# Dense products of a hybrid backbone step: upper and lower weight parts in two passes

## The chip, the core and the metric

The kernel runs on one core of one Trainium2 chip. The metric is device time in microseconds (us) of one execution. TensorE (PE in the profile, PEld for its weight loads) multiplies, VectorE (DVE), ScalarE (ACT) and GpSimd (POOL) work element by element, and SyncE (SP) issues nearly all transfers. Each engine works through its own instructions in order and waits on semaphores for the others.

## The reference, cut to what matters

One layer of a diffusion backbone for 128 context and 256 latent tokens, 384 columns in all, at width 1024 and in float32:

```python
h = _rmsnorm(x, p['norm_g'][0]) * (1.0 + sc1) + sh1
x = x + 0.5 * g1 * _swiglu(h, p['ffn_wi'][0], p['ffn_wo'][0])      # width 2816
h = _rmsnorm(x, p['norm_g'][1]) * (1.0 + sc2) + sh2
mix, states = _mixer_block(h, p, init, grid)                       # S5, SSD, gated DeltaNet
x = x + g2 * mix
h = _rmsnorm(x, p['norm_g'][2]) * (1.0 + sc3) + sh3
x = x + 0.5 * g3 * _swiglu(h, p['ffn_wi'][1], p['ffn_wo'][1])
```

The mixer projects `h` with `w_in` (the products' blocks of 128 columns), runs three scans in both directions, gates the branches and projects with `w_out`. Shifts, scales and gates come from SiLU(cond) @ `ada_w`.

## The kernel before

Activations lie transposed, features on the 128 partitions and the 384 tokens as columns (386 where two shift columns ride along). A dense product takes a weight tile of 128 output features by up to 8 slices of 128 input features from DRAM (`wraw`, three buffers) and splits it (`split_w`, lines 280 to 287): ACT casts it to the upper part `whi` in the fast float32r form (line 285), DVE subtracts that from the raw tile and leaves the lower part `wlo` (line 286). `whi` and `wlo` have two buffers each (`HLB`). Activations are split in the same way into `xh` and `xl` (`hh`/`hl`, `gh`/`gl`, and so on). `mm3` (lines 291 to 296) then adds three matmuls per slice k into one PSUM tile: upper weight by `xh` (line 294), upper weight by `xl` (line 295), lower weight by `xh` (line 296). A product of 8 slices is 24 matmuls.

There are 243 such products. In their order: the first FFN (`ffn(0, ...)`): per half of the 22 hidden blocks 22 products of `wi` (line 405; two to a block, multiplied on DVE at line 412) and 16 of `wo` (line 432; two to an output block, of 6 and 5 slices, added into `x` at line 434); then the mixer with 50 products of `w_in` (line 617) and one of small projections (line 631), 32 of the branches (line 1008) and 8 of `w_out` (line 1319); then the second FFN like the first. (Four more split tiles, of `wz`, lines 892 to 898, don't go through `mm3`.)

In the first FFN, DVE also computes the modulation vectors of later sections (line 272, a multiply with sum per 128x1024 tile) and tables for the S5 scan (lines 554 to 607, with a few transposes and matmuls on PE). In the mixer, DVE runs a recurrence of 31 steps (lines 828 to 838), PE transposes q, k and the convolved blocks through PSUM (`transposes`, line 695, two buffers that ACT empties, for q and k at line 825), and the inverses of the DeltaNet start with matmuls at lines 927 and 928, go on as small steps on DVE (lines 953 and 955), are written to DRAM (line 961) and read back (lines 1058 and 1060) for the matmuls at line 1045.

The order on each engine is not the order in which the code is written: the tile framework schedules by a simulated timeline, in which the next instruction that is ready goes first, and allots the buffers. So an edit in `mm3` can move instructions on every engine.

Of the kernel before, what the change touches and what calls it, by code (L numbers as in the profile page):

```python
# [22 lines left out]
KD = 8  # L23
# [118 lines left out]
def tile_hybrid(ctx: ExitStack, tc: tile.TileContext, a, o):  # L142
    nc = tc.nc
    V, S, G, PE = nc.vector, nc.scalar, nc.gpsimd, nc.tensor
# [32 lines left out]
    for q, names in enumerate((SMALL[:NFIRST], SMALL[NFIRST:])):  # L177
# [3 lines left out]
        for n in names:  # L181
            s = SMALL_SHAPES[n]
            w = int(np.prod(s))
# [104 lines left out]

    last_mm = [None]

    def mm3(pt, w, xh, xl, k0, nk, start, stop):
        hi, lo = w
        for k in range(nk):
            PE.matmul(pt, hi[:, k, :], xh[k0 + k], start=start and k == 0, stop=False)  # L294
            PE.matmul(pt, hi[:, k, :], xl[k0 + k], start=False, stop=False)  # L295
            last_mm[0] = PE.matmul(pt, lo[:, k, :], xh[k0 + k], start=False, stop=stop and k == nk - 1).ins  # L296

    def rsqrt(y, x, root=False):
# [93 lines left out]
    def ffn(f, xv, hh, hl, fill, rb=None, done=None, early=(), fill2=None):  # L392

        early = list(early)
        tw = T if rb is None else TW
        for part in range(2):
            gh, gl = blocks("gh", NH, FR), blocks("gl", NH, FR)
            for j in range(NH):  # L400
                m = part * NH + j
                pa, pb = ([psD, psD], [psD, psC], [psB, psB])[m if m < 3 else 0]
                pa, pb = pa([P, tw]), pb([P, tw])
                for w, pt in enumerate((pa, pb)):
                    mm3(pt, early.pop(0) if early else split_w(a["wi"][f, m, w], KD), hh, hl, 0, KD, True, True)
                sa = tmp.tile([P, T], F32, name="sa", tag="t384", bufs=NT3)
                g = tmp.tile([P, T], F32, name="g", tag="t384", bufs=NT3)
                if callable(rb):
                    rb = rb()
                if rb is None:  # L410
                    S.activation(sa, pa, AF.Silu)
                    V.tensor_tensor(g, sa, pb, op=ALU.mult)
                else:
                    V.tensor_tensor(sa, pa[:, 0:T], rb, op=ALU.mult)
                    V.tensor_tensor(g, pb[:, 0:T], rb, op=ALU.mult)
                    ba, bb = shifts(pa), shifts(pb)
                    for e, s0, s1 in HALVES:
                        S.activation(sa[:, s0:s1], sa[:, s0:s1], AF.Silu, bias=ba[:, e:e + 1])
                        V.scalar_tensor_tensor(g[:, s0:s1], g[:, s0:s1], bb[:, e:e + 1], sa[:, s0:s1],
                                               op0=ALU.add, op1=ALU.mult)  # L420
                S.copy(gh[j], g)
                last = V.tensor_tensor(gl[j], g, gh[j].bitcast(F32), op=ALU.subtract)
                with tc.issue_after(last.ins):
                    fill(m, g)
            if part == 0:
                gate = small.tile([P, KD, 2], F32, name="gate", tag="gate")
                V.tensor_scalar(gate, msec(2 if f == 0 else 8), 0.5, None, op0=ALU.mult)
            for m in range(KD):
                py = psd.tile([P, T], F32, name="ps_d", tag="ps_d")
                for k0, nk in ((0, 6), (6, 5)):  # L430
                    w = split_w(a["wo"][f, m, :, part * NH + k0:part * NH + k0 + nk], nk)
                    mm3(py, w, gh, gl, k0, nk, k0 == 0, k0 != 0)
                for e, s0, s1 in HALVES:
                    last = V.scalar_tensor_tensor(xv[m][:, s0:s1], py[:, s0:s1], gate[:, m, e:e + 1], xv[m][:, s0:s1],
                                                  op0=ALU.mult, op1=ALU.add)
                if fill2:
                    with tc.issue_after(last.ins):
                        fill2(part, m)
                if part == 1:
                    if m == 0:  # L440
                        acc = small.tile([P, T], F32, name="acc", tag="acc", bufs=1)
                    if f == 0 or m < KD - 1:
                        sq_add(acc, xv, m)
                    if done:
                        done(xv, m, acc)
        return acc
# [167 lines left out]

    def dense_in(blk, hh, hl, tw=T, ps=psD):
        pt = ps([P, tw])
        mm3(pt, split_w(a["win"][blk], KD), hh, hl, 0, KD, True, True)
        return pt

    def unscaled(dst, pt, rb):  # L620
# [80 lines left out]
    def mixer(es, xv, acc, xh, xl, sc):  # L701
# [53 lines left out]
        for m in range(4):  # L755
            pt = pts[m]
# [8 lines left out]
        hh, hl = modnorm(rb, sc, xv, 1)  # L765
# [33 lines left out]
        for which, tokt in ((1, ktok), (0, qtok), (2, vtok)):  # L799
            for m in range(4):  # L800
# [4 lines left out]
                pt = transposes([raw[:, X3[x]] for x in range(3)])  # L805
# [199 lines left out]

        def br(n, m, xh, xl):
            pt = psd.tile([P, T], F32, name="ps_d", tag="ps_d")
            mm3(pt, split_w(a["wbr"][m, n], 4), xh, xl, 0, 4, True, True)
            return pt

        def gates():
# [303 lines left out]
        for m in range(KD):  # L1315
            xo = t3("xo")
            nc.sync.dma_start(out=xo, in_=dX[m])
            py = psd.tile([P, T], F32, name="ps_d", tag="ps_d")
            mm3(py, split_w(a["wout"][m], KD), mgh, mgl, 0, KD, True, True)
            for e, s0, s1 in HALVES:  # L1320
                V.scalar_tensor_tensor(xv[m][:, s0:s1], py[:, s0:s1], gate2[:, m, e:e + 1], xo[:, s0:s1],
                                       op0=ALU.mult, op1=ALU.add)
# [110 lines left out]
```

## Time and profile before

| | us |
|---|---|
| median of 3 runs (1144.04 to 1144.78) | 1144.62 |
| profiled execution | 1144.53 |
| its span, first to last instruction | 1142.5 |
| PE busy | 1090.7 |
| PE weight loads busy | 1025.8 |
| DVE busy | 805.2 |
| ACT busy | 472.1 |
| POOL busy | 145.1 |

Matmuls are pipelined, so PE's busy time holds the end of one matmul beside the start of the next. Weight loads run beside the matmuls, one for each. The mean granted clock of TensorE is 0.987 of full speed.

### The profile page before, as it was taken

Reading aid. Unit: us, or ns where it says so; the run is one execution under the profiler, and the core shown is the slowest. Engines: PE = TensorE matmul, PEld = TensorE weight load, DVE = VectorE, ACT = ScalarE, POOL = GpSimd, SP = SyncE. Lnnn points to the kernel's source line nnn. Section 1 sums busy time; section 2 is a strip of 40 time slices with the busy share of each in tenths; the row PEclk is TensorE's granted clock in tenths of the full one; section 3 lists DMA queues with packets and bytes.
Section 4 is the critical chain, followed back from the end, with each engine's and each line's share of the span. In section 5 each row is a group of like instructions: output and inputs, shape, how many; then the busy total and the mean of one; then the engine's idle time right before and its main releaser. Section 6 shows DMA issues by size and latency. Waiting matters only on the chain.

```text
span 1142.5 us, 19011 instructions
## 1 busy us (share of the span) xinstructions
PE 1090.7 (95%) x7192; PEld 1025.8 (90%) x7192; DVE 805.2 (70%) x1652; ACT 472.1 (41%) x871; POOL 145.1 (13%) x135
## 2 busy tenths in 40 slices
PE   5999999999899999899899999999999999999996
PEld 2699899999899999799788888999899999999996
DVE  5699988899967759745554567786866974455554
ACT  5354323333355666743333232243444342334341
POOL 0000000000000100036172563116200000000000
PEclk9999999999999999899999999999999999999998
DMA  9787777576574653268646434456745634544342
GB/s 357 281 265 234 226 232 247 178 225 197 147 262 152 158 171 114 74 189 254 182 144 181 116 105 118 141 158 200 247 142 166 205 112 126 147 115 125 106 127 81
DMA packets 106731, 200.29 MB, mean 175 GB/s; under 512 B 34960, under 2 KB 60816, under 8 KB 106384
## 3 DMA queue, kind: packets, MB, share of 16 engines
q1 hardware_dynamic: 104336, 195.94, 55.7%
q10 hardware_dynamic: 2304, 3.15, 0.8%
q8 instruction: 56, 0.92, 0.3%
q14 instruction: 35, 0.29, 0.1%
HBM read 175.56 MB, written 23.49 MB: 174 GB/s over the span
## 4 chain that ended last, share of the span: by engine, by line
PE 78%; DVE 11%; ACT 3%; issue 3%; DMA 3%; SPq 1%; POOL 1%; DVEq 0%; ACTq 0%; POOLq 0%
PE ps_d L296 21%; PE ps_d L294 21%; PE ps_d L295 20%; DVE wlo L286 3%; ACT whi L285 1%; PE ps_s L979 1%; PE ps_c L1045 1%; PE ps_s L789 1%; PE ps_m L876 1%; PE ps_d L244 1%; DVE cv L687 1%; PE ps_s L1045 1%; DMA cb<-in_condr_dram 1%; DMA wraw<-in_wo_dram 1%; PE ps_m L222 1%
## 5 line engine op out<-in xcount | busy, mean ns | idle before, releaser
L285 ACT CAST whi<-wraw 128x1024 fp32r<-128x1024 f32 (+3 forms) x247 | 228.0, 924 | 450.5 <-PE ps_d L295 300.2
L286 DVE TENSOR_TENSOR wlo<-wraw,whi 128x1024 fp32r<-128x1024 f32 (+3 forms) x247 | 275.1, 1114 | 132.2 <-ACT whi L285 130.2
L294 PE MATMUL ps_d<-hh,whi 128*128 128x384 f32 x696 | 239.4, 345 | 9.9 <-ACT whi L285 6.7
L296 PE MATMUL ps_d<-hh,wlo 128*128 128x384 f32 x696 | 240.2, 346 | 1.3 <-DVE wlo L286 1.1
L295 PE MATMUL ps_d<-hl,whi 128*128 128x384 f32 x696 | 238.3, 343 | 0.9 <-DVE hl L382 0.9
L294 PEld LDWEIGHTS ps_d<-hh,whi 128*128 128x128 f32 x696 | 132.1, 190 | 18.8 <-ACT whi L285 9.9
L296 PEld LDWEIGHTS ps_d<-hh,wlo 128*128 128x128 f32 x696 | 132.2, 190 | 7.5 <-DVE wlo L286 4.1
L295 PEld LDWEIGHTS ps_d<-hl,whi 128*128 128x128 f32 x696 | 132.3, 190 | 3.5 <-DVE hl L382 2.2
L296 PE MATMUL ps_d<-gh,wlo 128*128 128x384 f32 x352 | 119.4, 340 | 3.7 <-DVE wlo L286 3.6
L296 PE MATMUL ps_d<-xh,wlo 128*128 128x386 f32 x352 | 119.7, 340 | 0.9 <-DVE wlo L286 0.9
L294 PE MATMUL ps_d<-gh,whi 128*128 128x384 f32 x352 | 119.0, 338 | 1.5 <-ACT whi L285 1.5
L294 PE MATMUL ps_d<-xh,whi 128*128 128x386 f32 x352 | 119.6, 340 | 0.0
L295 PE MATMUL ps_d<-xl,whi 128*128 128x386 f32 x352 | 119.4, 339 | 0.0
L295 PE MATMUL ps_d<-gl,whi 128*128 128x384 f32 x352 | 118.6, 337 | 0.0
L272 DVE SCALAR_TENSOR_TENSOR ajunk<-araw,cb 128x1024 bf16<-128x1024 f32 x80 | 97.4, 1218 | 2.6 <-ACT cb L264 2.6
L296 PEld LDWEIGHTS ps_d<-gh,wlo 128*128 128x128 f32 x352 | 66.0, 188 | 6.4 <-DVE wlo L286 5.6
L294 PEld LDWEIGHTS ps_d<-gh,whi 128*128 128x128 f32 x352 | 66.1, 188 | 2.7 <-ACT whi L285 2.5
L296 PEld LDWEIGHTS ps_d<-xh,wlo 128*128 128x128 f32 x352 | 66.2, 188 | 1.8 <-DVE wlo L286 1.8
L295 PEld LDWEIGHTS ps_d<-xl,whi 128*128 128x128 f32 x352 | 66.6, 189 | 0.0
L294 PEld LDWEIGHTS ps_d<-xh,whi 128*128 128x128 f32 x352 | 66.2, 188 | 0.0
L295 PEld LDWEIGHTS ps_d<-gl,whi 128*128 128x128 f32 x352 | 66.1, 188 | 0.0
L874 POOL TENSOR_TENSOR Atri<-smalls,dahl 128x512 fp32r<-128x512 f32 x36 | 40.8, 1150 | 61.2 <-DVE dahl L772 53.7
(464 smaller groups left out, 1736.2 us busy)
## 6 DMA issues: line engine op xcount, KB each, us to landing
wraw<-in_wi_dram SPq DMA_DIRECT2D x88, 512.0 KB
araw<-in_ada_dram SPq DMA_DIRECT2D x56, 512.0 KB
wraw<-in_win_dram SPq DMA_DIRECT2D x50, 512.0 KB
wraw<-in_wo_dram SPq DMA_DIRECT2D x32, 384.0 KB
wraw<-in_wo_dram SPq DMA_DIRECT2D x32, 320.0 KB
wraw<-in_ada_dram SPq DMA_DIRECT2D x16, 512.0 KB
wraw<-in_wbr_dram SPq DMA_DIRECT2D x32, 256.0 KB
re<-dM SPq DMA_DIRECT2D x24, 192.0 KB
```

What stands on the lines that cost most here:

```text
L222: PE.matmul(pt[32 * g:32 * g + 32, :], c32[:, k, :], raw[:, j, :], start=q < 2, stop=q >= 2, tile_position=(0, 32 * g))
L244: PE.matmul(pt[32 * g:32 * g + 32, :], c32[:, 4 * h + g, :], raw[:, g, :], start=h == 0, stop=h == 1, tile_position=(0, 32 * g))
L272: V.scalar_tensor_tensor(junk, raw, 1.0, cb[:, e], op0=ALU.mult, op1=ALU.mult, accum_out=t[:, b, e:e + 1])
L285: S.copy(hi, raw)
L286: V.tensor_tensor(lo, raw, hi.bitcast(F32), op=ALU.subtract)
L294: PE.matmul(pt, hi[:, k, :], xh[k0 + k], start=start and k == 0, stop=False)
L295: PE.matmul(pt, hi[:, k, :], xl[k0 + k], start=False, stop=False)
L296: last_mm[0] = PE.matmul(pt, lo[:, k, :], xh[k0 + k], start=False, stop=stop and k == nk - 1).ins
L687: V.scalar_tensor_tensor(rows(cv), ur[:, :, tap:tap + 64], w[:, tap:tap + 1], rows(cv), op0=ALU.mult, op1=ALU.add)
L789: PE.matmul(pt[:, ri, g], sw[:, ri, g], UU[:, 4 * b + g], start=True, stop=True)
L874: G.tensor_tensor(A, bc(INCL[d], [P, 4, P], 1), bc(dahl[:, w, x, 12 * d + c0:12 * d + c0 + 4], [P, 4, P], 2), op=ALU.mult)
L1045: PE.matmul(dst[r_, h], lh[r_, h], rh[r_, h] if len(rh.shape) == 3 else rh[r_], start=True, stop=True)
```

## The change

The three matmuls per slice are no longer issued together: `mm3` issues the two matmuls with the upper part for all slices, and then those with the lower part for all slices, into the same PSUM tile. With `late=True` it issues them as before. That is set where activations arrive slice by slice: the first six `wi` products of each FFN, the second `wo` product of output block 0 in each half, the first `w_in` product after the mixer's normalisation (block 14), and the first output block of each branch and of `w_out`. These are 22 of the 243 products; 221 change.

```diff
-    def mm3(pt, w, xh, xl, k0, nk, start, stop):
+    def mm3(pt, w, xh, xl, k0, nk, start, stop, late=False):
         hi, lo = w
-        for k in range(nk):
+
+        def upper(k):
             PE.matmul(pt, hi[:, k, :], xh[k0 + k], start=start and k == 0, stop=False)
             PE.matmul(pt, hi[:, k, :], xl[k0 + k], start=False, stop=False)
+
+        for k in range(nk):
+            upper(k)
+            if late:
+                last_mm[0] = PE.matmul(pt, lo[:, k, :], xh[k0 + k], start=False, stop=stop and k == nk - 1).ins
+        for k in range(0 if late else nk):
             last_mm[0] = PE.matmul(pt, lo[:, k, :], xh[k0 + k], start=False, stop=stop and k == nk - 1).ins
...
-                    mm3(pt, early.pop(0) if early else split_w(a["wi"][f, m, w], KD), hh, hl, 0, KD, True, True)
+                    mm3(pt, early.pop(0) if early else split_w(a["wi"][f, m, w], KD), hh, hl, 0, KD, True, True,
+                        late=part == 0 and m < 3)
...
-                    mm3(py, w, gh, gl, k0, nk, k0 == 0, k0 != 0)
+                    mm3(py, w, gh, gl, k0, nk, k0 == 0, k0 != 0, late=m == 0 and k0 > 0)
...
-        mm3(pt, split_w(a["win"][blk], KD), hh, hl, 0, KD, True, True)
+        mm3(pt, split_w(a["win"][blk], KD), hh, hl, 0, KD, True, True, late=blk == 14)
...
-            mm3(pt, split_w(a["wbr"][m, n], 4), xh, xl, 0, 4, True, True)
+            mm3(pt, split_w(a["wbr"][m, n], 4), xh, xl, 0, 4, True, True, late=m == 0)
...
-            mm3(py, split_w(a["wout"][m], KD), mgh, mgl, 0, KD, True, True)
+            mm3(py, split_w(a["wout"][m], KD), mgh, mgl, 0, KD, True, True, late=m == 0)
```

Every engine has the same instructions as before, but for two more loads of ACT's function tables near the start of the mixer. The order on PE in the first FFN, before, where the ninth product (`ps_d_817`, `whi_821`, `wlo_822`) begins behind the eighth (`ps_d_731`) and the tenth is `ps_d_818`, `whi_851`:

```order
L294 MATMUL ps_d_731<-hh_195,whi_764 128x384
L295 MATMUL ps_d_731<-hl_197,whi_764 128x384
L296 MATMUL ps_d_731<-hh_195,wlo_765 128x384
L294 MATMUL ps_d_817<-hh_194,whi_821 128x384
L295 MATMUL ps_d_817<-hl_196,whi_821 128x384
L294 MATMUL ps_d_818<-hh_194,whi_851 128x384
L295 MATMUL ps_d_818<-hl_196,whi_851 128x384
L296 MATMUL ps_d_817<-hh_194,wlo_822 128x384
L294 MATMUL ps_d_817<-hh_194,whi_821 128x384
```

Two upper matmuls of the tenth product stand ahead of the first lower one of the ninth; `whi_851` lies in the buffer of `whi_764`. The same place now, from the end of the ninth product's upper pass (lines 297 and 298 are the upper matmuls, 305 the lower):

```order
L298 MATMUL ps_d_817<-hl_197,whi_821 128x384
L297 MATMUL ps_d_818<-hh_194,whi_851 128x384
L298 MATMUL ps_d_818<-hl_196,whi_851 128x384
L297 MATMUL ps_d_818<-hh_194,whi_851 128x384
L298 MATMUL ps_d_818<-hl_196,whi_851 128x384
L297 MATMUL ps_d_818<-hh_194,whi_851 128x384
L298 MATMUL ps_d_818<-hl_196,whi_851 128x384
L297 MATMUL ps_d_818<-hh_194,whi_851 128x384
L298 MATMUL ps_d_818<-hl_196,whi_851 128x384
L305 MATMUL ps_d_817<-hh_194,wlo_822 128x384 x4
L305 MATMUL ps_d_817<-hh_195,wlo_822 128x384 x4
L297 MATMUL ps_d_818<-hh_195,whi_851 128x384
```

The lower pass of the ninth product (8 matmuls) now stands in the middle of the tenth's upper pass, with the whole upper pass of the ninth ahead of the tenth's first matmul. The second place is in the mixer, on PE, where q is transposed (`qtok`, 12 transposes) and two convolved blocks after it (`cv`). Before:

```order
L294 MATMUL ps_d<-hh,whi 128x384
L295 MATMUL ps_d<-hl,whi 128x384
L296 MATMUL ps_d<-hh,wlo 128x384
L695 MATMUL ps_m<-ident,qtok 128x128 x12
L695 MATMUL ps_m<-ident,cv 128x128 x6
L294 MATMUL ps_d<-hh,whi 128x384
```

The 18 transposes stood in a row. Now the first 8 of q are followed by a lower pass and a whole upper pass (16 matmuls, of which the first two stand here):

```order
L298 MATMUL ps_d<-hl,whi 128x384
L705 MATMUL ps_m<-ident,qtok 128x128 x8
L305 MATMUL ps_d<-hh,wlo 128x384 x8
L297 MATMUL ps_d<-hh,whi 128x384
L298 MATMUL ps_d<-hl,whi 128x384
```

and the last 4 of q and the two convolved blocks stand behind that upper pass:

```order
L298 MATMUL ps_d<-hl,whi 128x384
L705 MATMUL ps_m<-ident,qtok 128x128 x4
L305 MATMUL ps_d<-hh,wlo 128x384 x8
L989 MATMUL ps_s<-tw,UU 48x128
L705 MATMUL ps_m<-ident,cv 128x128 x3
L989 MATMUL ps_s<-tw,UU 48x128
L705 MATMUL ps_m<-ident,cv 128x128 x3
L297 MATMUL ps_d<-hh,whi 128x384
```

So the transposes now have dense matmuls between them.

## Rows read from the trace of the kernel before

**Rows 1.** The page's busy times: engine, us, share, instructions.
```profile
PE 1090.7 (95%) x7192; PEld 1025.8 (90%) x7192; DVE 805.2 (70%) x1652; ACT 472.1 (41%) x871; POOL 145.1 (13%) x135
```

**Rows 2.** Stretches: start:end, us; each engine's busy us; clock, DMA.
```profile
60.00:250.00 190.00, 184.33 (x1190) 178.58 (x1190) 175.32 (x280) 69.12 (x104) 0.00 (x0) 1.00 0.73 228
250.00:345.00 95.00, 90.88 (x602) 87.01 (x601) 81.37 (x153) 40.86 (x74) 1.46 (x3) 1.00 0.66 204
...
456.00:486.00 30.00, 25.24 (x172) 23.08 (x171) 22.66 (x61) 23.93 (x54) 0.95 (x1) 0.89 0.29 83
486.00:541.00 55.00, 55.00 (x463) 50.29 (x462) 28.38 (x72) 22.00 (x37) 25.86 (x26) 1.00 0.71 219
541.00:577.00 36.00, 31.04 (x226) 27.38 (x225) 20.70 (x71) 15.14 (x27) 4.82 (x5) 0.91 0.72 202
577.00:780.00 203.00, 203.00 (x1693) 179.98 (x1693) 134.95 (x267) 64.61 (x118) 78.82 (x69) 1.00 0.44 131
...
892.00:1130.00 238.00, 237.83 (x1350) 237.50 (x1348) 138.28 (x253) 86.11 (x126) 0.00 (x0) 1.00 0.43 127
```

**Rows 3.** Timeline at 73 us: start, us, instruction, idle before it and releaser.
```profile
72.92 1.05 ACT L285 CAST whi<-wraw 128x1024 fp32r<-128x1024 f32 x1 [2.73 <-PE ps_d L295]
...
74.01 0.19 PEld L294 LDWEIGHTS ps_d<-hh,whi 128*128 128x128 f32 x1 [0.93 <-ACT whi L285]
74.01 0.44 PE L294 MATMUL ps_d<-hh,whi 128*128 128x384 f32 x1 [0.61 <-ACT whi L285]
```

**Rows 4.** Waits, 60 to 345 us: who waited for whom: us, times, longest.
```profile
PEld ps_d L294 <- ACT whi L285: 8.5, 9, 1.3
PEld ps_d L296 <- DVE wlo L286: 6.0, 8, 1.8
...
ACT whi L285 <- DMA wraw<-in_wo_dram: 6.1, 2, 3.9
```

**Rows 5.** Waits of the weight loads, 345 to 382 us.
```profile
PEld ps_d L294 <- ACT whi L285: 2.4, 2, 1.5
PEld ps_d L296 <- DVE wlo L286: 1.2, 2, 0.7
```

**Rows 6.** Waits of the weight loads, 382 to 486 us.
```profile
PEld ps_m L695 <- ACT qT L825: 5.0, 3, 2.1
PEld ps_d L296 <- DVE wlo L286: 0.9, 1, 0.9
```

**Rows 7.** Waits of the weight loads, 780 to 892 us.
```profile
PEld ps_d L296 <- DVE wlo L286: 5.0, 9, 1.0
PEld ps_d L294 <- ACT whi L285: 0.6, 1, 0.6
```

**Rows 8.** DVE's subtractions by size (60 to 345 us; the last: all).
```profile
L286 DVE TENSOR_TENSOR wlo<-wraw,whi 128x1024 fp32r<-128x1024 f32 x41 | 50.0, 1220 | 8.9 <-ACT whi L285 8.9
L286 DVE TENSOR_TENSOR wlo<-wraw,whi 128x768 fp32r<-128x768 f32 x16 | 15.3, 956 | 5.5 <-ACT whi L285 5.3
L286 DVE TENSOR_TENSOR wlo<-wraw,whi 128x640 fp32r<-128x640 f32 x16 | 13.1, 820 | 0.0
...
L286 DVE TENSOR_TENSOR wlo<-wraw,whi 128x512 fp32r<-128x512 f32 x32 | 29.3, 916 | 12.2 <-ACT whi L285 10.8 <-ACT YF L1090 1.4
```

**Rows 9.** Timeline, 465 to 475 us, ACT's cast and PE behind the transposes.
```profile
465.97 1.05 ACT L285 CAST whi<-wraw 128x1024 fp32r<-128x1024 f32 x1 [2.48 <-PE ps_d L295]
...
473.90 0.52 PE L295 MATMUL ps_d<-hl,whi 128*128 128x384 f32 x1
474.22 0.52 PE L296 MATMUL ps_d<-hh,wlo 128*128 128x384 f32 x1
```

**Rows 10.** ACT's function table load, 382 to 486 us: us, mean ns.
```profile
L689 ACT ACT_TABLE_LOAD x1 | 1.3, 1283 | 0.0
```

**Rows 11.** Waits of the weight loads, 486 to 577 us.
```profile
PEld ps_s L1045 <- issue: 4.8, 1, 4.8
```

## The prediction

> **What bounds the kernel now.** I read the busy times first, then a table of stretches, then the waits of the tensor engine's weight loads stretch by stretch, then three places in the timeline. The page gives PE 1090.7 us of a 1142.5 us span and its weight loads (PEld) 1025.8 [rows 1]. The reader should see that PE sets the time nearly everywhere: from 892 to 1130 us it is busy 237.83 of 238 us, 1350 matmuls, 0.176 us each, without a wait, and from 577 to 780 us it is busy for all of 203 us [rows 2]. There nothing can be won by an order of the same matmuls. What can be won stands where PE waits, and the same table shows these stretches: 60 to 345 us (the first FFN), 456 to 486 and 541 to 577 us (the mixer).
>
> The waits are priced by the weight loads, whose idle time before a late load is nearly all that the wait costs: at 74.01 us the load stood idle for 0.93 us, while the matmul's own row counts 0.61, since the matmuls before it still drain [rows 3]. By these rows the waits for `whi` and `wlo` cost 8.5 + 6.0 us in the first FFN [rows 4], 2.4 + 1.2 between 345 and 382 us [rows 5], 0.9 between 382 and 486 [rows 6], 5.0 + 0.6 between 780 and 892 [rows 7]: 24.6 us in all. After 892 us there are none.
>
> **The change part by part.** No instruction is added or removed on PE, DVE, POOL or the queues; 221 of 243 products get their 8 (or 6, 5, 4) lower matmuls behind their upper ones, and the scheduler lays everything else round that. ACT alone gets two more table loads.
>
> *Waits for `whi`.* Before, the last upper matmul stands next to last in a product, so the buffer, one of two, comes free at a product's end. Eight of the nine waits in the first FFN have the form of rows 3: PE's order puts the first upper matmuls of the next product ahead of the lower ones of the present one, the cast for that next product starts only when the product before is through (ACT idle 2.73 us until then), takes 1.05 us, and PE has 0.35 us of work beside it. Now the buffer comes free after two thirds of a product, with 8 lower matmuls (1.4 us) and a whole upper pass (2.8 us) still ahead of the next but one product, against 1.05 us of cast. I cost these eight at nothing afterwards: minus 7.5 us of the 8.5. The ninth goes with a weight tile that lands late (ACT waited 3.9 us for one transfer [rows 4]); it stays.
>
> *Waits for `wlo`, first FFN.* The first lower matmul moves from third to at least seventeenth place in a product, 2.5 us later, and the subtraction takes 0.82 to 1.22 us [rows 8]. All 6.0 us could go. But DVE is busy 175.32 of 190 and 81.37 of 95 us there [rows 2]; where it falls behind for several microseconds a delay of 2.5 us is used up. Between nothing and 6.0 I take 4.0.
>
> *What the new order costs there.* A lower pass now stands up to 13 upper matmuls inside the next product, so its `wlo` buffer comes free up to 2.3 us later than before, and DVE, which works in order, can stand in front of the subtraction after next. Nothing in the trace of before shows such a wait: from 0 to the 28 us of idle time that DVE has there. I take 1.5 us, near the row that it is like, DVE's present idle time of a few tenths per subtraction. First FFN: 7.5 + 4.0 - 1.5 = 10.0.
>
> *345 to 382 us.* DVE's normalisation of the next input sets the end, and product 81, which takes its input slice by slice, keeps its order. Of 3.6 us I take 1.0.
>
> *382 to 486 us.* The wait for `wlo` (0.9) goes. The larger one is a wait for transposes: 18 in a row, for which ACT must empty PSUM, while ACT stands at a cast of `whi` (idle 2.48 us until PE frees the buffer) with the copies behind it [rows 9]. It costs 5.0 us [rows 6]. PE idles through most of 467 to 472 us, and behind that the clock stands at 1.2 and not 2.4 GHz (0.89 on the mean of 456 to 486 us [rows 2]): a dozen matmuls start 0.32 us apart and not 0.176 [rows 9], 1.7 us more. In the new order the 12 transposes of q stand as 8 and 4 with 8 lower and 16 upper matmuls between, and the two groups of cv behind another 8. ACT's copies into `Hc` still lie between, so I leave one wait of 2.1 us, the longest of the three [rows 6]: 5.0 + 1.7 - 2.1 = 4.6 less. The two table loads, 1.28 us each [rows 10], fall into a stretch where ACT is not full: between 0 and 2.6, I take 0.5. Together 0.9 + 4.6 - 0.5 = 5.0.
>
> *486 to 577 us.* PE waits 4.8 us for the inverses' blocks that come back from DRAM [rows 11]. They hang on a chain over PE, DVE and the queue that starts with PE's own matmuls at line 927, and PE had no wait from 486 to 541 us [rows 2]. So the chain moves with PE and the wait stays: 0.
>
> *577 to 780 us.* No wait before, so a new order can only add: 0 to the 4.8 us of the longest wait in the mixer; I take 1.5.
>
> *780 to 892 us.* 5.6 us of waits in ten places; about 1.0 at first products that keep their order. Of the rest I take two thirds, 3.0, since the subtraction of these smaller tiles is slow for its size (0.92 us for 512 columns, 0.82 for 640 [rows 8]).
>
> Sum: 10.0 + 1.0 + 5.0 + 0 - 1.5 + 3.0 = 17.5 us. The profiled execution took 1144.53 us (span 1142.5 and 2.0 around it), 0.1 below the median of the runs. So 1144.5 - 17.5 = **1127 us**.
>
> **A rule against the trace.** Rows 3 and 4 show one gap, 0.9 us, repeated eight times at a buffer of two. The Trainium skill, "Perfetto Trace Analysis", section Optimization Strategy, says that the same gap repeating on the engine that should be saturated can mean too few buffers for the next tile. By that rule, with the buffer count unchanged, the `whi` waits would stay; it is the fourth rival, which rows alone price. The trace agrees in part, since the cast does wait for a buffer; no run here shows yet whether an earlier release is enough.
> The same page, section Identifying the Most-Contended Engine, wants weight-load busy time and not matmul busy time for the room that is left. By PEld's busy time [rows 2] 11.4 + 8.0 = 19.4 us would be open in the first FFN, against 14.5 by the waits; an estimate from that rule would put the sum up to 5 us lower. I keep the waits, as small transposes also leave weight loads idle.
>
> **The rivals.**
> 1. *Given back.* The chain behind the 4.8 us wait does not move with PE (DVE's small steps set it), and all that was won before 541 us, 16.0 us, lengthens that wait. 1144.5 - (3.0 - 1.5) = 1143. For it: the wait is there. Against it: PE's row of 55.00 of 55 us.
> 2. *Slower: DVE becomes the bound of the first FFN.* Its idle time from 60 to 345 us is 28.3 us [rows 2], over 73 subtractions [rows 8] 0.39 us each. If each stands 0.6 us before a lower pass that came late, DVE needs 256.7 + 44 = 301 us for 285: 16 us more in place of 10 less, 1144.5 + 16 - 7.5 = 1153. It decides from 0.39 us per subtraction on, and the kernel is slower from (28.3 + 7.5)/73 = 0.49. Against it: each subtraction has a whole upper pass more to be late in.
> 3. *The lower pass is no slack.* The scheduler lays it where it expects `wlo` to be ready, so waits for `wlo` stay and only those for `whi` and the transposes go: 7.5 + 0.5 + 4.6 + 0.3 = 12.9, less 3.0 for new ones: 1135. For it: orders such as "8 upper, lower pass, 8 upper".
> 4. *Too few buffers.* The `whi` waits stay, those for `wlo` go: 4.0 + 0.5 + 0.9 + 3.0, and half of the transposes' 6.7, less 3.0 for new ones: 8.7, so 1136. Against it: the release is earlier by 1.4 us in rows of the order.
>
> **How the numbers follow.** Forecast 60%, given back 8%, DVE the bound 8%, no slack 12%, buffers 12%. Two tenths of a per cent, 2.3 us, is about what a measurement of this kernel can tell from no change. Of the forecast's case nearly all, and of rivals 3 and 4 most, lie below 1142.3: faster 82%, within 9% (rival 1 and the weak end of 3 and 4), slower 9%. The low end takes all `whi` and `wlo` waits (24.6) and the transposes' 6.7 less 3.0 for new ones: 28.3, so 1116. The high end, 1141, takes in rivals 3 and 4 with their own new waits and leaves out rivals 1 and 2.
>
> **What would show it.** Right: from 60 to 345 us the weight loads' waits for `whi` fall from 8.5 to about 1 us and for `wlo` from 6.0 to about 2; the last matmul of that FFN comes some 10 us earlier; the transposes of q wait under 2.5 us and the clock stays at 2.4 GHz behind them; the wait of the inverses stays near 4.8 us; 0.176 us per matmul after 892 us. Wrong: a wait of the inverses above 10 us (rival 1); DVE idle in front of subtractions with a lower pass of PE as releaser (rival 2); `wlo` waits above 5 us (rival 3) or `whi` waits above 5 (rival 4) in the first FFN; a matmul pitch other than 0.176 us, which would overthrow the ground of it all.

## The result, and the profile after

The changed kernel takes 1120.58 us (median of 4, 1118.55 to 1122.34), the kernel before 1144.61 beside it: a ratio of 0.979 (0.978 to 0.980), 24.0 us less. The forecast was 1127 us in a range of 1116 to 1141.

The busy times first. Against [rows 1] nothing was added on any engine but two instructions on ACT, and PE's work is the same; what fell is the span, 1142.5 to 1116.4 us.

```profile
PE 1075.8 (96%) x7192; PEld 1022.4 (92%) x7192; DVE 797.9 (71%) x1652; ACT 479.1 (43%) x873; POOL 145.7 (13%) x135
```

To see where, I compare the two traces at equal work: each matmul counts with the median pitch of its width in the trace before, and the table gives how much earlier the changed kernel reaches the same sum. The bounds are the stretches of the prediction, in the time of before. The count is good to about 1 us: the same kernel profiled a second time (experiment 12) comes out 0.8 us apart in the first FFN.

| stretch before (us) | bound after | forecast | measured |
|---|---|---|---|
| 0 to 60 | 60.2 | 0 | +0.2 |
| 60 to 345 (first FFN) | 335.5 | -10.0 | -9.7 |
| 345 to 382 | 369.1 | -1.0 | -3.4 |
| 382 to 486 | 466.7 | -5.0 | -6.4 |
| 486 to 577 | 555.3 | 0 | -2.4 |
| 577 to 780 | 759.6 | +1.5 | +1.3 |
| 780 to 892 | 867.7 | -3.0 | -3.9 |
| 892 to the end | 1116.4 | 0 | -1.8 |
| sum | | -17.5 | -26.1 |

The profiled execution is the fastest of the four (1118.55), 2.0 us under their median; so 26.1 here and 24.0 in the medians. The same stretches in the table of stretches (start:end, length; busy us of PE, PEld, DVE, ACT, POOL; clock, DMA share, GB/s), to lay beside [rows 2]:

```profile
60.00:336.00 276.00, 271.94 (x1793) 266.68 (x1794) 254.90 (x431) 111.18 (x177) 1.46 (x3) 1.00 0.72 227
336.00:370.00 34.00, 32.69 (x191) 32.00 (x190) 28.31 (x84) 21.74 (x46) 0.00 (x0) 1.00 0.73 153
370.00:467.00 97.00, 95.67 (x642) 94.01 (x641) 75.74 (x184) 74.77 (x211) 6.05 (x5) 1.00 0.45 145
467.00:556.00 89.00, 83.69 (x694) 76.68 (x694) 49.13 (x141) 39.44 (x63) 32.33 (x30) 0.95 0.73 218
```

The clock column is 1.00 from 60 to 467 us; before, it fell to half once at 372 us and once behind the transposes. The waits of the weight loads in the first FFN, 60 to 336 us (who waited for whom: us in total, times, longest):

```profile
PEld ps_d L297 <- ACT whi L285: 5.3, 4, 2.0
...
PEld ps_s L303 <- DVE wlo L286: 0.8, 1, 0.8
```

No lower matmul of a product in two passes (line 305) waits for `wlo` there; the one line left is a product in the old order, and it stands in the kernel before too. `whi` still costs 5.3 us, but in four waits and not nine, and three of them (4.4 us) are of another kind. ACT's own waits in the same stretch name it:

```profile
ACT whi L285 <- DMA wraw<-in_wo_dram: 22.5, 10, 4.8
```

Before, ACT waited twice for such a transfer, 6.1 us [rows 4]; now ten times, 22.5. One of them in the timeline at 295 us (start, us, engine, instruction, idle time before it and its releaser):

```profile
290.97 3.23 SPq L617 DMA_DIRECT2D dT<-tK  x4
...
292.34 1.69 DVE L286 TENSOR_TENSOR wlo<-wraw,whi 128x640 fp32r<-128x640 f32 x2
...
295.31 0.89 SPq L283 DMA_DIRECT2D wraw<-in_wo_dram  x2
...
299.80 0.83 ACT L285 CAST whi<-wraw 128x768 fp32r<-128x768 f32 x1 [4.83 <-DMA wraw<-in_wo_dram]
...
300.68 0.19 PEld L297 LDWEIGHTS ps_d<-gh,whi 128*128 128x128 f32 x1 [1.40 <-ACT whi L285]
300.68 0.44 PE L297 MATMUL ps_d<-gh,whi 128*128 128x384 f32 x1 [1.09 <-ACT whi L285]
```

The transfer is issued 4.5 us before the cast. The raw buffer that it needs is freed by the first of DVE's two subtractions, at 293.16 us; for the 2.15 us from there to its issue it stands behind other transfers on SyncE. Seven of the ten are issued within 0.2 us of the subtraction that frees their buffer. With PE no longer late, the weight tile itself is what comes late.

The fourth wait is still one of the old kind. At 147.5 us a product of `wo` that keeps its order ends late, and only 2 matmuls stand between the old tile of a buffer and its new one:

```profile
146.61 0.83 ACT L285 CAST whi<-wraw 128x768 fp32r<-128x768 f32 x1 [2.61 <-PE ps_d L298]
...
147.50 0.19 PEld L297 LDWEIGHTS ps_d<-gh,whi 128*128 128x128 f32 x1 [0.89 <-ACT whi L285]
```

In the later stretches the waits of the weight loads are these (336 to 370, 370 to 467, 467 to 556, 556 to 760, 760 to 868 us; the lines that matter of each):

```profile
PEld ps_d L298 <- DVE hl L391: 1.0, 1, 1.0
PEld ps_d L297 <- ACT whi L285: 0.7, 1, 0.7
...
PEld ps_m L705 <- ACT cv L699: 1.0, 1, 1.0
...
PEld ps_m L705 <- ACT qT L835: 0.2, 1, 0.2
...
PEld ps_s L1055 <- POOL Lm L1063: 5.3, 1, 5.3
...
PEld ps_d L297 <- ACT sgate L1035: 1.6, 1, 1.6
...
PEld ps_d L303 <- DVE wlo L286: 1.8, 2, 1.6
```

The transposes of q wait 0.2 us where they waited 5.0 [rows 6]; the inverses' wait is 5.3 where it was 4.8 [rows 11]; a new wait of 1.6 stands in the stretch whose longest was 0.8; the waits for `wlo` after 760 us fell from 5.0 in nine [rows 7] to 1.8 in two, both at a product in the old order (line 303).

### The profile page after: what moved, and what is told of

Read it like the earlier page. It is cut to its first block, busy times and chain, and to the rows that moved or that the text cites. A ratio compares the mean times of both kernels' runs of the same rounds, so it can differ in the third digit from the quotient of the medians.

```text
span 1116.4 us, 18986 instructions
## 1 busy us (share of the span) xinstructions
PE 1075.8 (96%) x7192; PEld 1022.4 (92%) x7192; DVE 797.9 (71%) x1652; ACT 479.1 (43%) x873; POOL 145.7 (13%) x135
## 4 chain that ended last, share of the span: by engine, by line
PE 81%; DVE 7%; DMA 5%; ACT 3%; issue 2%; SPq 1%; POOL 1%; DVEq 0%; ACTq 0%; POOLq 0%
PE ps_d L297 22%; PE ps_d L298 22%; PE ps_d L305 20%; DVE wlo L286 2%; PE ps_d L303 1%; DMA wraw<-in_win_dram 1%; ACT whi L285 1%; DMA wraw<-in_wo_dram 1%; PE ps_c L1055 1%; DMA wraw<-in_wi_dram 1%; PE ps_s L989 1%; PE ps_s L1055 1%; PE ps_m L886 1%; PE ps_s L799 1%; DMA X<-dI 1%
## 5 line engine op out<-in xcount | busy, mean ns | idle before, releaser
L286 DVE TENSOR_TENSOR wlo<-wraw,whi 128x1024 fp32r<-128x1024 f32 (+3 forms) x247 | 269.4, 1097 | 77.9 <-ACT whi L285 55.3
L305 PE MATMUL ps_d<-hh,wlo 128*128 128x384 f32 x664 | 133.7, 339 | 0.0
L305 PEld LDWEIGHTS ps_d<-hh,wlo 128*128 128x128 f32 x664 | 116.2, 188 | 0.7 <-issue 0.4
L444 DVE SCALAR_TENSOR_TENSOR x<-ps_d,gate,x 128x128 f32<-128x128 f32 x64 | 23.9, 412 | 57.7 <-PE ps_d L305 49.8
L305 PE MATMUL ps_d<-gh,wlo 128*128 128x384 f32 x332 | 64.9, 338 | 0.0
L305 PE MATMUL ps_d<-xh,wlo 128*128 128x386 f32 x328 | 64.2, 338 | 0.0
L305 PEld LDWEIGHTS ps_d<-gh,wlo 128*128 128x128 f32 x332 | 58.2, 188 | 0.6 <-issue 0.4
L305 PEld LDWEIGHTS ps_d<-xh,wlo 128*128 128x128 f32 x328 | 58.3, 189 | 0.0
```

Of the source, the lines that this page charges most:

```text
L286: V.tensor_tensor(lo, raw, hi.bitcast(F32), op=ALU.subtract)
```

## The experiments

Each kernel was timed beside the kernel before. What a stretch won is counted by equal work, as above, from one profiled execution of each kernel. The diffs are cut to the lines that matter, and some are written shorter than in the kernel.

**1. Two passes in the FFNs alone.** The mixer's calls get `late=True`:

```diff
-        mm3(pt, split_w(a["win"][blk], KD), hh, hl, 0, KD, True, True, late=blk == 14)
+        mm3(pt, split_w(a["win"][blk], KD), hh, hl, 0, KD, True, True, late=True)
```

> Two passes in the products of the two FFNs alone; the mixer's 91 products keep three matmuls per slice. Theory (each stretch wins by its own waits): the first FFN ends 9.7 us earlier as in the changed kernel and the second FFN adds under 1, the mixer's waits stay as before (transposes 5.0, products with gates 5.6): 10 us less, 1134.5 us. Rival (the mixer wins because it starts earlier and is laid out anew, whatever its own products look like): most of the 24 us, 1123 us. Second rival (what the FFN wins is given back at the inverses' wait, which then is 4.8 + 10 us): 1144 us.

Measured: 1138.64 us (ratio 0.995, 0.993 to 0.996), 4 us above the theory, 5 below the second rival and 16 above the first. Its waits decide against both rivals. The first FFN won 6.5 us (a spell at half clock at 303 us took back 1.5), the transposes waited as before, and the wait of the inverses was 3.6 us: nothing of what the FFN won was given back there.

```profile
PEld ps_m L705 <- ACT qT L835: 5.0, 3, 2.1
...
PEld ps_s L1055 <- POOL Lm L1063: 3.6, 1, 3.6
```

Another spell at half clock, 14 matmuls from 384 us, cost 2.6 us more in the mixer.

**2. Two passes in the mixer alone.** The same in the two calls of `ffn`:

```diff
-                        late=part == 0 and m < 3)
+                        late=True)
...
-                    mm3(py, w, gh, gl, k0, nk, k0 == 0, k0 != 0, late=m == 0 and k0 > 0)
+                    mm3(py, w, gh, gl, k0, nk, k0 == 0, k0 != 0, late=True)
```

> Two passes in the mixer's products alone; both FFNs keep three matmuls per slice. Theory: the first FFN keeps its waits for whi (8.5 us) and wlo (6.0), the mixer wins what it won in the changed kernel between 345 and 892 us (3.4 + 6.4 + 2.4 - 1.3 + 3.9 = 14.8 us by equal work of the tensor engine): 1130 us. Rival (the gain in the mixer came from the FFN's order at its entry): under 8 us, 1137 us or more.

Measured: 1129.29 us (0.986, 0.984 to 0.988). From 345 to 892 us it won 14.8 us, and nearly the same stretch by stretch as the changed kernel (-3.4 to 382 us, -5.7 from 460 to 486, -2.2 from 486 to 500). The mixer's gain belongs to the mixer's own products. The first FFN (60 to 345 us) kept its waits:

```profile
PEld ps_d L297 <- ACT whi L285: 7.5, 8, 1.3
PEld ps_d L303 <- DVE wlo L286: 6.1, 9, 1.8
```

**3. A third buffer for `whi`, old order.** In the first FFN, behind the first tiles, every third tile's `whi` lies in a buffer of the pool next door (`more` holds that pool during the first FFN, and the count of tiles):

```diff
-        hi, lo = into or (wst.tile([P, nk, w], FR, name=n, tag=n, bufs=HLB) for n in ("whi", "wlo"))
+        more[1] += 1
+        xp = more[0] if more[1] % 3 == 0 else None
+        if xp and not into:
+            into = [(xp if n == "whi" else wst).tile([P, nk, w], FR, name=n, tag=n, bufs=1 if n == "whi" else HLB)
+                    for n in ("whi", "wlo")]
+        hi, lo = into or (wst.tile([P, nk, w], FR, name=n, tag=n, bufs=HLB) for n in ("whi", "wlo"))
```

> The kernel before, three matmuls per slice, with a third buffer for whi in the first FFN (every third tile's whi lies in it). Theory (two separate waits): the waits for whi between 60 and 345 us fall from 8.5 to the one behind a late transfer, about 1, those for wlo stay at 6.0 or grow by some of it, since the subtractions come no earlier: 5 to 7 us less, 1138.5 us. Rival (one cause, too few buffers: with the third buffer the subtraction starts earlier too and both waits go): 12 us less or more, 1132.5 us. Second rival (the wait is only moved to the subtraction, which is the bound): no change, 1144 us.

Measured: 1141.47 us (0.997, 0.995 to 0.998), midway between the theory (1138.5) and no change (1144); 4.1 us in the first FFN. The weight loads from 60 to 343 us:

```profile
PEld ps_d L302 <- DVE wlo L292: 6.8, 7, 1.9
PEld ps_d L300 <- ACT whi L291: 3.9, 4, 1.9
```

Two separate waits, then: a buffer more takes more than half of the waits for `whi` (the theory had left 1 us of them, 3.9 stayed), and none of those for `wlo`, which grow a little. The rule of the Trainium skill weighed above (one gap repeated can mean too few buffers, "Perfetto Trace Analysis", section Optimization Strategy) holds for the one wait; what it names was worth 4.1 us here, where the change won 9.7.

**4. Upper by `xl` as the last pass.** Here `whi` is held to a product's end, as before; only the lower matmuls come late (`mm(w, x, k)` is one matmul of `mm3`).

```diff
-        for k in range(nk):
-            upper(k)
...
+        for k in range(nk):
+            mm(hi, xh, k, start=start and k == 0, stop=False)
+        for k in range(nk):
+            mm(lo, xh, k, start=False, stop=False)
+        for k in range(nk):
+            last_mm[0] = mm(hi, xl, k, start=False, stop=stop and k == nk - 1).ins
```

> The changed kernel with another order of the passes: upper by xh for all slices, lower by xh for all, upper by xl for all. The lower matmuls still come 8 places later than slice by slice, but whi is in use to the end of the product, as in the kernel before. Theory: in the first FFN the waits for wlo stay gone (under 1.5 us) and the waits for whi come back to 8.5 us or somewhat above; that FFN wins 5 of the 9.7 us, the whole kernel 1127 us. Rival (only the earlier release counts): the first FFN wins nothing, 1133 us or more. Second rival (only the late lower pass counts): as the changed kernel, 1121 us.

Measured: 1125.59 us (0.983, 0.981 to 0.984), and my theory fell, though its number (1127) was near: the first FFN won 10.1 us, all of it, and the waits for `whi` did not come back (61 to 337 us):

```profile
PEld ps_d L297 <- DVE wlo L286: 2.3, 2, 1.2
PEld ps_d L297 <- ACT whi L285: 1.4, 3, 0.8
```

So the earlier release is not what took these waits away. The order on PE tells what did. In the kernel before, only 3 matmuls stand between the last one with the old tile of a buffer and the first with its new tile: in the first order shown under the change they are the last lower one of `ps_d_731` and two of `ps_d_817`. Here they are the 8 of the next product's first pass. The wait was 0.93 us behind 3 matmuls (0.53 us), so a cast is ready 1.46 us after the release, and 8 matmuls (1.41 us) hide all but 0.05 us of it; the eight loads that come behind 8 stand idle for 0.06 to 0.11 us. What this kernel still lacks against the changed one lies in the mixer (a wait of 2.6 us at the transposes of q, and three spells at half clock from 361 to 402 us).

**5 and 6. The lag instead of the passes.** That gives a dose: the lower matmul of slice k stands behind the upper two of slice k+2, or k+1.

```diff
-        for k in range(nk):
-            upper(k)
-        for k in range(0 if late else nk):
-            last_mm[0] = PE.matmul(pt, lo[:, k, :], xh[k0 + k], start=False, stop=stop and k == nk - 1).ins
+        lag = 0 if late else 2
+        for k in range(nk):
+            upper(k)
+            if k >= lag:
+                lower(k - lag)
+        for k in range(max(nk - lag, 0), nk):
+            lower(k)
```

> The changed kernel with no two passes but a lag: the lower matmul of slice k stands behind the upper two of slice k+2 (the last two lower ones at the end). Theory after the last experiment (a wait for whi is as long as the cast minus the present product's matmuls that stand ahead of the next product's first one: 2 before, 8 with xl last, here 6, so 0.70 us more cover; and a wait for wlo shrinks by the 4 places, 0.70 us, that the first lower matmul comes later): in the first FFN the eight buffer waits for whi keep 1.9 us together, the one behind a transfer its 1.0, those for wlo 1.7 of 5.6 us; that FFN wins 9 us, nearly all of what two passes win, and the whole kernel takes 1125 us. Rival (the whole product must be parted, a lag of two slices does little): 1136 us. Second rival (the early release at the end of the upper pass is what counts: here whi comes free only two matmuls earlier than before): waits for whi above 5 us, 1133 us.

> The lower matmul of slice k stands behind the upper two of slice k+1. Theory (the cast for the next tile but one starts when the last matmul with the old tile is done and is ready 1.46 us later: 0.93 us of wait behind 3 matmuls before; behind 8 or more, as with xl last, with a lag of two and in two passes, no wait): here 6 matmuls, 1.06 us, lie between, so 0.4 us is left of each of the eight buffer waits of the first FFN, 3.2 us, beside 1.0 behind a transfer; the waits for wlo fall by two places (0.35 us) each to 3.5 us. That FFN wins 7 us and the kernel takes 1129 us. Rival (any lag at all breaks the pattern, as the lag of two did): 1126 us, no whi waits of this form. Second rival (the lag must reach the cast's whole length, or nothing is won): waits for whi of 8 us, 1136 us.

Measured: a lag of two 1125.84 us (0.983, 0.981 to 0.986), a lag of one 1128.22 us (0.984, 0.982 to 0.986). The timeline of the lag of one at 72 us: the last matmul with the old tile starts at 71.76, the cast starts when it is done, six matmuls follow, and the load for the seventh waits 0.41 us; 0.40 was forecast.

```profile
71.76 0.34 PE L303 MATMUL ps_d<-hl,whi 128*128 128x384 f32 x1
...
72.13 1.05 ACT L285 CAST whi<-wraw 128x1024 fp32r<-128x1024 f32 x1 [2.72 <-PE ps_d L303]
...
73.24 0.19 PEld L302 LDWEIGHTS ps_d<-hh,whi 128*128 128x128 f32 x1 [0.41 <-ACT whi L285]
```

Seven such waits in the first FFN lie between 0.41 and 0.52 us. With a lag of two 9 matmuls lie between (three of them lower ones behind the last upper one; I had counted 6), and none of this form is left at the products of `wi`. The waits of the lag of two (61 to 337 us), then of the lag of one (60 to 339 us):

```profile
PEld ps_d L299 <- DVE wlo L286: 2.9, 4, 1.1
PEld ps_d L302 <- ACT whi L285: 1.7, 3, 0.7
```

```profile
PEld ps_d L299 <- DVE wlo L286: 4.8, 6, 1.3
PEld ps_d L302 <- ACT whi L285: 3.7, 10, 0.5
```

The dose in one table, first FFN only, the matmuls between at the places that waited before:

| order | matmuls between | first lower matmul | waits for `whi` | for `wlo` | won |
|---|---|---|---|---|---|
| slice by slice | 3 | 3rd | 8.5 | 6.0 | 0 |
| lag of one | 6 | 5th | 3.7 | 4.8 | 6.7 |
| `xl` last | 8 | 9th | 1.4 | 2.3 | 10.1 |
| lag of two | 9 | 7th | 1.7 | 2.9 | 10.4 |
| two passes | 16 or more, once 2 | 17th or later | 5.3 (4.4 behind transfers) | 0 | 9.7 |

The shorter casts of `wo` bear the count out. They take 0.83 us and not 1.05, so by the same sum they are ready 1.24 us after the release: 2 matmuls between should leave 0.89 us, 3 leave 0.71, 6 leave 0.19. Measured are 0.89 (the changed kernel, above), 0.71 and 0.76 (before), and 0.20 to 0.25 (lag of one). The longest wait before, the 1.3 us of [rows 4], has a single matmul between, for which 1.28 us are due with a cast of 1.05 us; it took 1.28.

The lag of two wins as much there as two passes. What it lacks is the mixer: PE's transposes of q wait as they did, and the half clock stands behind them again, 10 matmuls from 460.6 us (370 to 475 us):

```profile
PEld ps_m L707 <- ACT qT L837: 4.6, 3, 2.8
```

**7. The fourth raw buffer.** Two passes, and in the first FFN every fourth raw tile in a buffer more (`more` as in experiment 3):

```diff
-        raw = wst.tile([P, nk, w], F32, name="wraw", tag="wraw", bufs=RAWB)
+        more[1] += 1
+        xp = more[0] if more[1] % 4 == 0 else None
+        raw = (xp or wst).tile([P, nk, w], F32, name="wraw", tag="wraw", bufs=1 if xp else RAWB)
```

> The changed kernel with a fourth buffer for the raw weights in the first FFN. Theory (what is left of the waits for whi there, 5.3 us in four, hangs on transfers that start late, because the raw buffer comes free only with a late subtraction): the waits behind transfers of wo at 160 and 301 us (1.0 and 1.4 us) go, the others stay or shrink: 2 to 3 us less than the changed kernel, 1118 us. Rival (the transfers are late for the queue's or the memory's sake): as the changed kernel, 1120.6 us, with the same waits. Second rival (DVE's late subtraction then shows as a wait for wlo): the whi waits go, as much comes for wlo, 1120.6 us.

Measured: 1116.33 us (0.975, 0.973 to 0.978), with experiment 9 the best kernel here. ACT's waits for those transfers fell from 22.5 to 4.5 us, and the weight loads' for `whi` from 5.3 to 0.9, with 0.9 new for `wlo`:

```profile
PEld ps_d L303 <- ACT whi L291: 0.9, 1, 0.9
PEld ps_d L311 <- DVE wlo L292: 0.9, 2, 0.6
...
ACT whi L291 <- DMA wraw<-in_wo_dram: 4.5, 2, 2.7
```

The first FFN won 13.5 us against 9.7. So the transfers were late for the buffer's sake. The 0.9 us for `whi` that are left are the wait of the old kind, behind 2 matmuls. The changed kernel was not timed beside this one; its medians were 1120.6 and 1120.1.

**8. No exceptions.** All five calls pass `late=False`, as here:

```diff
-        mm3(pt, split_w(a["win"][blk], KD), hh, hl, 0, KD, True, True, late=blk == 14)
+        mm3(pt, split_w(a["win"][blk], KD), hh, hl, 0, KD, True, True, late=False)
```

> The changed kernel with two passes in all 243 products, the 22 with slice-by-slice inputs too. Theory (there the lower matmuls fill the gaps between slices): the first FFN's products before 56 us end 4 to 7 us later, since 40 lower matmuls (7.0 us) come only behind the last slice; w_in block 14 and the branches lose some tenths, the first product of wout wins up to 1.6 us: 1125 us. Rival (the gaps are long enough that the exceptions don't matter): 1119.5 us.

Measured: 1124.38 us (0.982, 0.980 to 0.985). By 60 us it stood 5.3 us behind the changed kernel, and the loads' waits for slices of `hh` were 9.0 us and not 4.6:

```profile
PEld ps_d L297 <- ACT hh L390: 9.0, 4, 2.5
```

The first product of `w_out` won nothing; its wait of 1.6 us went over to its input.

**9. That product alone in two passes, with the fourth raw buffer.**

```diff
-            mm3(py, split_w(a["wout"][m], KD), mgh, mgl, 0, KD, True, True, late=m == 0)
+            mm3(py, split_w(a["wout"][m], KD), mgh, mgl, 0, KD, True, True)
```

> As the run with a fourth raw buffer in the first FFN, and the first product of w_out in two passes as well (it is the one place behind 780 us where the changed kernel still waits for wlo, 1.6 us). Theory: 1.6 us less than with the fourth buffer alone, 1116.5 us. Rival (its inputs come slice by slice, and the lower matmuls filled those gaps): 1118 us or more.

Measured: 1116.66 us (0.976, 0.973 to 0.978). That is the theory's number, but only because the fourth buffer alone takes 1116.33 and not the 1118 it reckoned with; against that nothing was won, and the rival's reason holds. In place of 1.6 us for `wlo` stand 1.6 us for the activations, which come slice by slice:

```profile
PEld ps_d L304 <- DVE mgl L1324: 1.6, 2, 1.3
```

**10. A lag of two, but two passes for `w_in`.** The lag becomes an argument, 2 unless given:

```diff
-        mm3(pt, split_w(a["win"][blk], KD), hh, hl, 0, KD, True, True, late=blk == 14)
+        mm3(pt, split_w(a["win"][blk], KD), hh, hl, 0, KD, True, True, late=blk == 14, lag_=KD)
```

> A lag of two slices in all products but those of w_in, which run in two passes. Theory (what a lag of two leaves on the table against two passes, 5 us, lies at the transposes of q, which a parted w_in product keeps apart): waits of the transposes under 1 us in place of 4.6, no low clock behind them, 5.5 us less than with the lag alone: 1120.5 us. Rival (the difference is spread over all products): 1124 us or more.

Measured: 1123.55 us (0.980, 0.978 to 0.983), between the two. The transposes' wait did fall to 0.2 us and no half clock stood behind them, as the theory said; but between 382 and 400 us the kernel lost 3.8 us at half clock, in a place without a wait (under the hardware, below).

**11. A lag of two in the FFNs, two passes in the mixer (`lag_=KD` in its three calls), the fourth raw buffer of experiment 7.**

> Two passes in all products of the mixer, a lag of two slices in both FFNs, and the fourth raw buffer in the first FFN. Theory (lag and passes are worth the same in the FFN, and the fourth buffer takes the transfers' waits from either): as the changed kernel with the fourth buffer, 1116.3 us. Rival (a shorter lag leaves DVE's subtractions less room, and the waits for wlo come back in the FFN, 2 to 3 us): 1119 us.

Measured: 1121.62 us (0.980, 0.977 to 0.982), 2.6 us above even the rival, and no better than the changed kernel without the fourth buffer, timed beside it (1120.12). With the transfers out of the way the longer distance of two passes counts after all, as the waits for `wlo` from 62 to 337 us say, 3.4 against 0.9 us:

```profile
PEld ps_d L305 <- DVE wlo L292: 3.4, 4, 1.6
```

The first FFN won 11.1 and not 13.5 us; that is 2.4 of the 6.1 us between the two profiled spans, and the rest is spread (1.0 before 60 us, 1.1 from 345 to 892, 1.7 behind) and not explained.

**12. The changed kernel again.**

> The changed kernel once more, unchanged, beside the last variants. Theory: 1120.6 us, with 5.3 us of waits for whi in the first FFN and 5 us at the inverses again. Rival (part of the 24 us hangs on how transfers fell in the first measurement): above 1123 us.

Measured: 1120.12 us (1118.01 to 1125.98), with 6.3 us of waits for `whi` in the first FFN and 5.6 at the inverses. The 24 us do not hang on the first measurement.

## Why the prediction was right

The changed kernel came 6.4 us under the forecast, inside the range. What the sum lacked lies behind 345 us, in terms put too low or at nothing.

**First FFN, 10.0 forecast, 9.7 measured.** The sum was right by luck, for its terms were not. For `whi` I took 7.5 and 3.2 came, because transfers of the raw tiles were late next (4.4 of the 5.3 us left); for `wlo` I took 4.0 of 6.0 and all 6.0 came; the 1.5 for subtractions that stand before a late lower pass did not come at all, so DVE never became the bound (rival 2). Two misses of opposite sign, 4.3 too much and 3.5 too little, made a sum of 9.2. I had seen one transfer late (the ninth wait) and not asked what the others would do once PE no longer hid them.

**The step that failed in its reason: "Now the buffer comes free after two thirds of a product".** That is so in the order, but it isn't needed. With `whi` held to the end of the product the waits went as well (experiment 4), and the lags show what they obey: the matmuls between the last use of the old tile and the first of the new one, 0.93 us of wait behind 3, 0.41 behind 6, 0.06 to 0.11 behind 8, none behind 9. The second half of that sentence, the matmuls "still ahead of the next but one product", was the right reason. Rival 4 is out, as the waits went with the buffers as they were; experiment 3 gives what a buffer is worth, 4.1 us.

**345 to 382 us, 1.0 forecast, 3.4 measured.** Waits fell from 3.6 to 1.7 us; and I overlooked that the clock would stay up. In the trace before it stood at half from 371.7 to 375.1 us, behind the waits there (columns as above):

```profile
371.70:375.10 3.40, 2.92 (x10) 2.85 (x10) 3.40 (x11) 1.79 (x6) 0.00 (x0) 0.50 0.92 124
```

That term was missing: seven dense matmuls at 0.32 us and not 0.176 are 1.0 us by themselves. With the 1.9 us of waits that makes 2.9 of the 3.4.

**382 to 486 us, 5.0 forecast, 6.4 measured.** The mechanism was right: with dense matmuls between, the transposes of q wait 0.2 us, and the half clock behind them is gone. I had left 2.1 us of wait in, ten times too much. Experiments 2 and 10 hold this gain with the old order or the lag in the FFN, experiments 1 and 5 lose it.

**486 to 577 us, 0 forecast, 2.4 measured.** The wait moved with PE, as I said (4.8, now 5.3), which ends rival 1. The 2.4 us come again in experiment 2 (2.8), so they go with the mixer's order. Nearly all of them, 2.2 us, lie between 486 and 500 us, in every kernel whose transposes of q wait less, and experiments 1, 3 and 5 (the lag of two), where those wait as before, have nothing there. In this stretch PE runs another mixture of small matmuls, for which the median pitch is a rough count. What they are stays open.

**577 to 892 us.** The 1.5 lost was a guess between 0 and 4.8, and its nearness to the 1.3 measured is luck; one new wait of 1.6 us for a gate stands there. The 3.0 won were 3.9: 5.6 us of waits became 1.8, all of it at products that kept their order. Rival 3 falls with these rows: no lower pass waits for `wlo`.

**After 892 us, 0 forecast, 1.8 measured.** There is no wait to win. Matmuls of 386 columns start 175.7 ns apart and not 177.5, on the mean of some 816, which makes 1.5 us. It goes with the second FFN's order in the main: the three kernels with the old order there have 177.0 to 177.5 ns, five of the six with two passes there 175.6 or 175.7 (experiment 1: 176.4), and those with a lag or with `xl` last anything from 175.7 to 177.7. Why is not explained.

## What to carry to other kernels

Where tiles rotate through two buffers, count the instructions that the consumer has between its last use of a buffer's old tile and its first use of the new one: their time has to cover release, refill and semaphore, and an order that pulls the next tile's first instruction forward spends that cover. A lag of two slices between parts that become ready at different times bought as much here in the first FFN as parting them wholly, though not in the mixer; and the longer distance paid again there (13.5 against 11.1 us) once the next bottleneck, the raw buffer, was removed. And once the waits of an engine are gone, look at what its supplier now waits for: that is the next edit, and here it was worth another 4 us.

## What the hardware showed that I had not expected

The clock of TensorE can fall where PE has no wait. In experiment 10, PE was busy from 371 to 381 us without a gap, in a run of matmuls of 48 and 36 columns with three transposes, and the clock fell from full to half at 375.1 us (columns as in the table of stretches above):

```profile
371.00:375.00 4.00, 4.00 (x36) 4.00 (x34) 3.97 (x10) 3.96 (x8) 1.22 (x1) 1.00 0.71 245
375.00:381.00 6.00, 6.00 (x28) 5.90 (x28) 1.73 (x4) 5.43 (x17) 3.87 (x4) 0.51 0.72 222
```

The changed kernel runs nearly the same matmuls in the same place (20 of 48 columns, 12 of 36, three transposes, then more of 48 columns), with the same last waits ahead of it (0.4 and 0.9 us, in experiment 10 0.3 and 1.0 us), and its clock stayed up:

```profile
371.00:376.40 5.40, 5.40 (x50) 5.40 (x49) 3.46 (x8) 4.79 (x11) 3.13 (x3) 1.00 0.84 251
```

Such spells come and go between kernels that do nearly the same there: at 382 us in experiment 1, at 388 and 398 in 4, at 375 and 389 in 10. PE had no wait there, and each of the five came within a run of 32 matmuls of 48 columns (some with other small ones between) or within 0.7 us of its end. Each of the 14 traces has four such runs, so 51 of 56 passed without one. They cost 1 to 3 us each. (The spell at 303 us in experiment 1 is another thing; a wait of 1.9 us stands ahead of it.)

The executions of one kernel scatter by 0.7 to 8 us. The mean granted clock, which is on record for each execution, is on the whole lower where the time is longer: of the nine executions of the kernel before beside experiments 10 to 12, the two longest (1149.4 and 1149.7 us) have the lowest clock, 0.981 and 0.982, and the shortest (1142.4) has one of the two highest, 0.987. That spells at half clock make much of the scatter fits this, but was not shown, since a trace belongs to one execution.
